# An RWKV-7 and convolution block on one core: the program writes TensorE's order itself, and a step of the recurrence takes both heads in one product

## The chip, the core and the metric

The kernel runs on one NeuronCore of a Trainium2 chip. Five engines work beside each other: TensorE (PE, matrix products; PEld is its weight load), VectorE (DVE), ScalarE (ACT), GpSimd (POOL) and SyncE (SP, which here only issues DMAs). Each runs its own instructions in the order in which they stand in the program, and waits on semaphores for the others. The metric is the device time of one execution in microseconds (us), as the median of several runs.

## The reference, cut to what matters

One block over 512 tokens and 1024 channels. Cut down, with the names of the reference:

```python
h = rms_norm(x, pre_mix_norm)
p_r, p_k, p_v, p_c, z_rwkv, z_conv = split(h @ w_in)          # 1024 x 7168
# RWKV-7: 16 heads of 64 channels; per token and head, with a state S (64 x 64):
sa = S @ a_t
S = S * w_t + outer(sa, b_t) + outer(v_t, k_t)
y = S @ r_t                                                    # a scan over 512 tokens
y_rwkv = (group_norm(y) + bonus) * g @ w_rwkv_out
# convolution: 31 taps along the tokens, one filter per channel
c = conv31(u * sigmoid(gate)); y_conv = silu(layer_norm(c)) @ w_conv_out
x = x + rms_norm((sigmoid(z_rwkv) * y_rwkv + sigmoid(z_conv) * y_conv) @ w_out)
h = rms_norm(x)
x = x + rms_norm((silu(h @ ffn_w_gate) * (h @ ffn_w_up)) @ ffn_w_down)
```

## The kernel before

Channels lie on the partitions in 8 tiles of 128 (two heads each), tokens on the free axis. A **dense product** is one 128-channel tile of an output: each operand is split into a high and a low part in fp32r, so that for each of the 8 k-tiles there are three matmuls of 128x512 (`acc3`, L179 to L181), 24 in all, into a PSUM tile `dn`. The weights come by DMA in halves (`wload`); ACT and DVE or POOL split them into `wh` and `wl`.

The scan is done in chunks of 64 tokens, for one channel tile ct (heads E and O, on partitions 0 to 63 and 64 to 127) after another. Everything of the recurrence is in plain fp32, for which one matmul in the code is two passes of TensorE; the profile counts passes. Per channel tile:

- `plan_decay`, `plan_keys`, `plan_recept`: decay, keys and receptance (`zw`, `za`, `ss`, `bck` on TensorE), then the operands `AR` and `bk`, and `bkT` by transposes (`tps`).
- `plan_inner`: 16 products `gps` give the masked matrices inside the chunks, `Mt` and `GR`.
- `plan_solve`: the inverse of I - M. DVE transposes `Mt` into `Mo` (L622), takes 31 steps of two instructions (`tt`, L634, and `Ps`, L638), and transposes back into `P` and `P32T` (L650). Small products of 32x32 (`wps`, `xps`) join the blocks; ACT writes the result into `Pbd`.
- `plan_values`: `vps`, `bps`, and the buffers `UV` and `SV`.
- `plan_chain`: the recurrence over the 8 chunks. A chunk is a row of steps in which TensorE's product goes through ACT to the next one: `zt` from `SV` and `AR`, ACT copies it to `zs` (L721), `zt` from `zs` and `Pbd`, ACT copies to `UV` (L738), `zt` from `UV` and `bkT` (and the old state through the identity), ACT scales it into the next `SV` (L751). Each product stands there twice, for E and for O, in a part of TensorE's array: `128*64` in the profile is an operand of 128 rows and 64 columns, `64*64` one of 64 and 64, `128*128` the whole array. The output `yp` of a chunk takes four more.
- `plan_finish`: group norm, bonus and gate (`ssy`, `bcy`, `gp`).

The convolution's 31 taps per channel tile are DVE instructions of 128x512 (`ca`, L844). After the scan come the gates, `w_ro`, `w_co` (operand `CH`), then the output projection (operand `MH`) and the feed-forward part (`FHH`, `FH`).

What sets the order: each piece of work is put into a list with a nominal time (`at`, with `PERIOD`, `CHT`, `CHP`, `CHS`, `SOLVE` and so on), the list is sorted, and the code is emitted in that order. Below it a scheduling layer orders the instructions of every engine once more, at build time, by its own estimate of when each is ready. Solve steps and taps are tied to each other on DVE in the order of emission.

Of the kernel before, what the change touches and what calls it, by code (L numbers as in the profile page):

```python
# [32 lines left out]
# nominal positions that order the program  # L33
PERIOD = 44.0
NCL = 3
CPERIOD = 96.0
CPERIOD2 = 20
DTZ = 0.25
CONV0 = 60
TG_ = 25  # L40
WBF = 4
T0P = 0.0
T1P = 475
TE0 = -26.0
TN0 = -10
DTC = 0.3
POST = 8
TZO = 20
LEAD = 11
DTF = 0.9  # L50
SOLVE = 25.0
CH0 = -2
CHP = 5.5
CHS = 0.9
# [44 lines left out]
def tile_hybrid_block(ctx, tc, xT, cst, prm, dwp, wl1, w2g, w_in, w_ro, w_co, w_o,  # L99
# [3 lines left out]
    PE = nc.tensor  # L103
# [96 lines left out]
    def bcast2(ps, r8, rx):  # L200
        S.activation(out=rx.rearrange("p (a v) -> p a v", v=HD),
                     in_=r8.unsqueeze(2).to_broadcast([P, 8, HD]), func=AF.Copy)
        bcast(ps, lambda b: rx[:, b * P:(b + 1) * P])

    # 1 / sqrt(v) for v > 0: a first guess from the bits, then Newton's steps
# [19 lines left out]
    def all_rstd(ps_all, eps, blocks=4):  # L225
        red = sp.tile([P, blocks], F32, tag="st", bufs=6, name="red")
        V.tensor_reduce(out=red, in_=ps_all[:, :, :, 0], axis=AX.X, op=ALU.add)
        r = rstd_from(red, eps, blocks)
# [44 lines left out]
    # mean square of x over the channels, per token  # L273
# [10 lines left out]
    # the first products take x before its norm, and the norm after them  # L284
# [26 lines left out]
    # derived parameters  # L311
# [25 lines left out]
    # low-rank inputs: (h + (h_prev - h) mu) W = h (W - mu W) + h_prev (mu W)  # L337
# [17 lines left out]
    def low_rank(g):  # L355
        t_ = low[g]
        lo_f = tmp("lo_f", "th") if g else ep_.tile([P, T], F32, name="lo_f")
        if g == 0:
            pa, pb_ = (pm.tile([P, T], F32, tag=g_, bufs=1, name="lora") for g_ in ("sb", "fi"))
            for k in range(NT):  # L360
                for q, ps in ((0, pa), (2, pb_)):
                    acc3(ps, t_[:, q, k, :], t_[:, q + 1, k, :], [k], lambda k: XH[:, k, :],
                         lambda k: XL[:, k, :], k == 0, k == NT - 1)
            sh = tmp("sh", "sq", 2)
            V.tensor_mul(lo_f, pa, bx)
            V.tensor_mul(sh, pb_, bx)
            V.tensor_add(lo_f[:, 1:T], lo_f[:, 1:T], sh[:, 0:T - 1])
            S.activation(out=lo_f[E], in_=lo_f[E], func=AF.Tanh)
            # the low parts beside the high ones, under the other half of the rows
            for X, R, Q in ((LH, E, O), (LL, O, E)):  # L370
                S.activation(out=X[R], in_=lo_f[R], func=AF.Copy)
                V.tensor_sub(X[Q], lo_f[R], f(X[R]))
        else:
            ps = pd.tile([P, T], F32, tag="dn", name="lora")
            for k in range(NT):
                for q, rh, rl in ((0, hh, hl), (2, hhs, hls)):
                    acc3(ps, t_[:, q, k, :], t_[:, q + 1, k, :], [k], rh, rl,
                         k + q == 0, k == NT - 1 and q == 2)
            S.activation(out=lo_f, in_=ps, func=AF.Tanh, scale=0.5)
            S.activation(out=lo_f, in_=lo_f, func=AF.Identity, scale=0.5, bias=0.5)  # L380
            split(lo_f, GH, GL)

    def open_loop():
# [3 lines left out]
        for j in range(2):  # L387
            t_ = kp.tile([P, NCH, L], F32, tag=f"Pbd{j}", bufs=1, name=f"Pbd{j}")
            G.memset(t_, 0.0)
            Pbd.append(t_)  # L390
# [20 lines left out]
    def low2(ps, h_, l_, R, X):  # L411
        PE.matmul(ps, lhsT=h_, rhs=X, start=True, stop=False)
        PE.matmul(ps, lhsT=l_[R], rhs=X[R], start=False, stop=True)

    st = [{} for _ in range(NT)]
    plan = []
# [7 lines left out]
    solved, tapped = [None], [None]  # L424

    halves = []

    def plan_dense(t0, dt, wap, then, rh=hh, rl=hl):
# [5 lines left out]
        def mm(k):  # L434
            if k == 0:
                d["ps"] = pd.tile([P, T], F32, tag="dn", name="dn")
            k0 = k // WK * WK
            wh, wl = d[k0]
            j = k - k0
            cols = slice(j * P, (j + 1) * P)  # L440
            acc3(d["ps"], wh[:, cols], wl[:, cols], [k], rh, rl, k == 0, k == NT - 1)

        for k0 in range(0, NT, WK):
            ts = [t0 + 3 * dt * k for k in range(k0, k0 + WK)]
            fns = [lambda k=k: mm(k) for k in range(k0, k0 + WK)]
            if k0 + WK == NT:
                ts.append(t0 + 3 * dt * NT)
                fns.append(lambda: then(d["ps"]))
            halves.append([ts, lambda eng, k0=k0: load(k0, eng), fns])

    # weights are loaded ahead of their use, as far as the buffers go
    def plan_halves():
        halves.sort(key=lambda e: e[0][0])
        for i, (ts, ld, fns) in enumerate(halves):
            t_ = ts[0] - LEAD
            if i >= WB:
                t_ = max([t_] + [e[0][WK - 1] + 0.001 for e in halves[:i - WB + 1]])
            at(0, t_)(lambda ld=ld, i=i, t_=t_: ld(G if T0P < t_ < T1P else None))
            late = max(t_ + 0.001 - ts[0], 0.0)
            ts[:] = [t + late for t in ts]  # L460
            for t, fn in zip(ts, fns):
                at(0, t)(fn)

    at(0, -36.0)(load_rest)
    at(0, -35.0)(lambda: low_weights(0))
    at(0, -30.0)(lambda: low_rank(0))
    at(0, TN0)(normed)
    at(0, 0.0)(open_loop)
    at(0, 4.0)(lambda: low_weights(1))
    at(0, TG_)(lambda: low_rank(1))  # L470

    DT = PERIOD / 72 * DTF
    DL = 24 * DT
    CHT = max(2 * DL + 14.0 + SOLVE, 3 * DL + 4.0) + CH0

# [7 lines left out]
    def plan_decay(ct):  # L483
        s_ = st[ct]

        @at(ct, 0.0)
        def _():
            w2h, w2l = low_out(ct, 0, 2 * P, "w2")
            # decay: log w = -exp(-1/2) sigmoid(z)
            zw = pm.tile([P, T], F32, tag="sm", name="zw")  # L490
            low2(zw, w2h[:, 0:P], w2l[:, 0:P], E, LH)
            cum = ktmp("cum")
            S.activation(out=cum, in_=zw, func=AF.Tanh, scale=0.5, bias=der(D_W0H, ct))
            S.activation(out=cum, in_=cum, func=AF.Identity, scale=0.5, bias=0.5)
            V.tensor_tensor_scan(out=cum, data0=reset, data1=cum, initial=0.0,
                                 op0=ALU.mult, op1=ALU.add)
# [687 lines left out]
```

## Time and profile before

| | |
|---|---|
| three runs | 1139.59, 1144.58, 1146.76 us; median 1144.58 |
| profiled execution, first to last instruction | 1165.1 us |
| busy: PE, DVE, ACT, POOL | 1138.6, 721.4, 616.5, 96.2 us |
| mean granted TensorE clock of the profiled execution | 0.950 |

The profiled execution has no time of its own outside the profiler; its span, 1165.1 us, stands 1.8% above the median of the runs without a profile. A clock of 1.00 is 2.4 GHz, 0.50 is 1.2 GHz, the two levels that are granted. Matmuls overlap in TensorE, so that the time of one more matmul is seen from the distance of two starts and not from its length.

### The profile page before, as it was taken

Reading aid. Unit: us, or ns where it says so; the run is one execution under the profiler, and the core shown is the slowest. Engines: PE = TensorE matmul, PEld = TensorE weight load, DVE = VectorE, ACT = ScalarE, POOL = GpSimd, SP = SyncE. Lnnn points to the kernel's source line nnn. Section 1 sums busy time; section 2 is a strip of 40 time slices with the busy share of each in tenths; the row PEclk is TensorE's granted clock in tenths of the full one; section 3 lists DMA queues with packets and bytes.
Section 4 is the critical chain, followed back from the end, with each engine's and each line's share of the span. In section 5 each row is a group of like instructions: output and inputs, shape, how many; then the busy total and the mean of one; then the engine's idle time right before and its main releaser. Section 6 shows DMA issues by size and latency. Waiting matters only on the chain.

```text
span 1165.1 us, 17942 instructions
## 1 busy us (share of the span) xinstructions
PE 1138.6 (98%) x6506; PEld 869.8 (75%) x6506; DVE 721.4 (62%) x1699; ACT 616.5 (53%) x1291; POOL 96.2 (8%) x140
## 2 busy tenths in 40 slices
PE   7999999999999999999999999999999999999996
PEld 5777675757676767677788788899888888888886
DVE  7968676747776748699698737546444444433324
ACT  6777776758756747564655724535333333333321
POOL 0111010101010101112222000000000000000000
PEclk9999988869988869899999999999999999999998
DMA  7145342524342423356798434500332322333322
GB/s 245 44 100 118 78 98 46 116 46 92 71 100 50 97 69 81 68 125 147 163 203 197 117 99 139 178 19 10 101 98 91 99 91 94 96 91 109 109 64 73
DMA packets 74202, 117.41 MB, mean 101 GB/s; under 512 B 15745, under 2 KB 21249, under 8 KB 74113
## 3 DMA queue, kind: packets, MB, share of 16 engines
q1 hardware_dynamic: 58848, 88.47, 25.2%
q0 software_dynamic: 15264, 27.79, 14.3%
q8 instruction: 51, 0.84, 0.3%
q14 instruction: 39, 0.31, 0.1%
HBM read 84.25 MB, written 2.10 MB: 74 GB/s over the span
## 4 chain that ended last, share of the span: by engine, by line
PE 91%; ACT 4%; DVE 3%; issue 1%; DMA 0%; SPq 0%; DVEq 0%; ACTq 0%
PE dn L179 22%; PE dn L181 22%; PE dn L180 22%; PE gps L589 3%; PE yp L759 2%; PE zt L726 2%; PE zt L718 2%; PE vps L695 1%; PE zt L744 1%; PE yp L763 1%; PE bps L704 1%; PE ss L194 1%; PE psf L180 1%; PE psf L179 1%; PE psf L181 1%
## 5 line engine op out<-in xcount | busy, mean ns | idle before, releaser
L159 ACT ACTIVATE wh<-wf 128x512 fp32r<-128x512 f32 (+1 forms) x172 | 106.6, 621 | 245.5 <-PE dn L180 237.8
L160 DVE TENSOR_TENSOR wl<-wf,wh 128x512 fp32r<-128x512 f32 (+1 forms) x172 | 116.0, 676 | 136.1 <-ACT wh L159 136.1
L179 PE MATMUL dn<-HH,wh 128*128 128x512 f32 x408 | 173.0, 426 | 0.8 <-DVE cpad L823 0.5
L844 DVE SCALAR_TENSOR_TENSOR ca<-cpad,dw,ca 128x512 f32<-128x512 f32 x240 | 171.8, 744 | 1.4
L180 PE MATMUL dn<-HL,wh 128*128 128x512 f32 x408 | 172.1, 422 | 0.0
L181 PE MATMUL dn<-HH,wl 128*128 128x512 f32 x408 | 171.1, 420 | 0.0
L170 POOL DMA_DIRECT2D wl<-wf x106 | 91.6, 870 | 505.3 <-ACT wl L169 325.6
L181 PE MATMUL dn<-FHH,wl 128*128 128x512 f32 x320 | 127.0, 397 | 0.0
L179 PE MATMUL dn<-FHH,wh 128*128 128x512 f32 x320 | 126.6, 395 | 0.0
L180 PE MATMUL dn<-FHL,wh 128*128 128x512 f32 x320 | 125.8, 393 | 0.0
L168 ACT ACTIVATE wh<-wf 128x512 fp32r<-128x512 f32 x106 | 66.3, 629 | 69.1 <-PE dn L180 68.1
L179 PEld LDWEIGHTS dn<-HH,wh 128*128 128x128 f32 x408 | 78.9, 194 | 18.9 <-issue 0.7
L181 PEld LDWEIGHTS dn<-HH,wl 128*128 128x128 f32 x408 | 78.6, 193 | 17.6 <-issue 0.5
L180 PEld LDWEIGHTS dn<-HL,wh 128*128 128x128 f32 x408 | 79.0, 194 | 16.4 <-issue 0.4
L180 PEld LDWEIGHTS dn<-FHL,wh 128*128 128x128 f32 x320 | 60.2, 188 | 15.0
L181 PEld LDWEIGHTS dn<-FHH,wl 128*128 128x128 f32 x320 | 60.1, 188 | 14.5
L179 PEld LDWEIGHTS dn<-FHH,wh 128*128 128x128 f32 x320 | 60.0, 188 | 13.8
L169 ACT ACTIVATE wl<-wh 128x512 fp32r<-128x512 f32 x106 | 66.3, 628 | 2.1 <-ACT UV L738 0.4
L179 PE MATMUL dn<-FH,wh 128*128 128x512 f32 (+1 forms) x166 | 64.3, 387 | 0.0
L181 PE MATMUL dn<-FH,wl 128*128 128x512 f32 (+1 forms) x166 | 64.1, 386 | 0.0
L180 PE MATMUL dn<-FH,wh 128*128 128x512 f32 (+1 forms) x166 | 64.1, 386 | 0.0
L638 DVE TENSOR_TENSOR Ps<-Ps,tt 128x60 f32<-128x60 f32 (+24 forms) x248 | 52.6, 212 | 3.4
(303 smaller groups left out, 2111.0 us busy)
## 6 DMA issues: line engine op xcount, KB each, us to landing
wf<-in_w_in_dram SPq DMA_DIRECT2D x112, 256.0 KB, 3.1
wl<-wf POOLq DMA_DIRECT2D x106, 256.0 KB, 3.7
wf<-in_w_gt_dram SPq DMA_DIRECT2D x44, 256.0 KB, 2.6
wf<-in_w_up_dram SPq DMA_DIRECT2D x44, 256.0 KB, 2.8
wf<-in_w_dn_dram SPq DMA_DIRECT2D x40, 256.0 KB, 2.7
wf<-in_w_ro_dram SPq DMA_DIRECT2D x16, 256.0 KB, 3.0
wf<-in_w_co_dram SPq DMA_DIRECT2D x16, 256.0 KB, 2.6
wf<-in_w_o_dram SPq DMA_DIRECT2D x16, 256.0 KB, 2.9
```

What stands on the lines that cost most here:

```text
L159: S.activation(out=hi, in_=src, func=AF.Copy)
L160: V.tensor_sub(lo, src, f(hi))
L168: S.activation(out=wh, in_=wf, func=AF.Copy)
L169: S.activation(out=wl, in_=f(wh), func=AF.Copy, scale=-1.0)
L170: G.dma_start(out=wl, in_=wf, accum_op=ALU.add)
L179: PE.matmul(ps, lhsT=a, rhs=rh(k), start=first and j == 0, stop=False)
L180: PE.matmul(ps, lhsT=a, rhs=rl(k), start=False, stop=False)
L181: PE.matmul(ps, lhsT=b, rhs=rh(k), start=False, stop=last and j == n - 1)
L589: PE.matmul(ps[:, c, :], lhsT=bk[R, hc * 4 + c, :], rhs=AR[R, hc * 4 + c, par:par + 2, :], start=True, stop=True)
L638: solved[0] = V.tensor_add(Ps[:, 0:j, q0:8], Ps[:, 0:j, q0:8], tt)
L718: PE.matmul(zt[R, 0, :], lhsT=AR[:, c, 2 * par, :], rhs=SV[:, c, par, :], start=True, stop=True)
L844: a_ = V.scalar_tensor_tensor(out=o_, in0=cb[:, j:j + T], scalar=tap(j), in1=o_, op0=ALU.mult, op1=ALU.add)
```

## The change

1. All matmuls from the start of the recurrence to the merge get a dependency on the one before them (class `Pinned`), so that TensorE's order is the order in which the code emits them and nothing moves it. `Pinned` also adds up a nominal TensorE clock `PE.t`.
2. The list of nominal times is gone. Each channel tile has generators (`prep`, `values`, `chain`, `taps`, `finish`), which yield a delay or an event to wait for; `Weave` resumes whichever is due at `PE.t`, and otherwise emits the three matmuls of one k-tile of a dense product whose weights are taken to be loaded.
3. A chain step takes both heads in one product of the whole array: `AR` holds both heads' operands next to each other, `Pbd` is block-diagonal with 128 columns, and the state comes out as two 64-column halves, of which ACT takes the diagonal blocks. ACT copies `zs` in two instructions where it was one.
4. The outputs `yp` are taken after chunk 4 and after chunk 8 instead of in each chunk.
5. `zw` and `za` use full-height low parts, padded with zeros. The 32 `gps` passes of a tile come after the solve of the tile before it, where they could begin earlier. `low_rank` of the gate stands ahead of the first keys.

```diff
+    class Pinned:
+        on, last, t, mode = False, None, 0.0, None
+        def _pin(self, i, lhsT, rhs, tr=False):
+            if self.on and self.last is not None:
+                order(i, self.last)
+            self.last = i
...
+            if self.mode not in (None, mode):
+                self.t += 0.12
...
-    def at(ct, t):
-        def add(fn):
-            plan.append((ct * PERIOD + t, len(plan), fn))
-            return fn
-        return add
+    class Weave:
...
+        def run(self):
+            while True:
+                if self.heap and self.heap[0][0] <= PE.t:
+                    self.step(heapq.heappop(self.heap)[2])
+                    continue
+                self.feed()
+                if self.loaded and self.loaded[0][0] <= PE.t:
+                    units = self.loaded[0][1]
+                    units.pop(0)()
...
-            zt = pc.tile([P, 3, L], F32, tag="ch", name="zt")
-            for par, R in ((0, E), (1, O)):
-                PE.matmul(zt[R, 0, :], lhsT=AR[:, c, 2 * par, :], rhs=SV[:, c, par, :],
-                          start=True, stop=True)
-            zs = sp.tile([P, L], F32, tag="zs", name="zs")
-            S.activation(out=zs, in_=zt[:, 0, :], func=AF.Copy)
...
+            zt = pc.tile([P, 5, L], F32, tag="ch", name="zt")
+            PE.matmul(zt[:, 0:2, :], lhsT=AR[:, c, 0:2, :], rhs=SV[:, c, :, :],
+                      start=True, stop=True)
+            zs = sp.tile([P, L], F32, tag="zs", name="zs")
+            for par, R in ((0, E), (1, O)):
+                S.activation(out=zs[R], in_=zt[R, par, :], func=AF.Copy)
+            yield HOP
+            PE.matmul(zt[:, 2, :], lhsT=pb[:, c, :], rhs=zs, start=True, stop=True)
...
+                if c > 0:
+                    PE.matmul(zt[:, 3:5, :], lhsT=ident, rhs=SV[:, c, :, :],
+                              start=True, stop=False)
+                PE.matmul(zt[:, 3:5, :], lhsT=bkT[:, c, :], rhs=UV[:, c, :, :],
+                          start=c == 0, stop=True)
...
+            if c == NCH // 2 - 1:
+                yp = s_["yp"] = py.tile([P, NCH, L], F32, tag="y", name="yp")
+                outputs(range(0, NCH // 2))
+            if c < NCH - 1:
+                yield HOP
+        outputs(range(NCH // 2, NCH))
...
+        if ct:
+            yield ("solve", ct - 1), 0.0
+        Mt = kp.tile([P, NCH, L], F32, tag="Mt", bufs=BUFS[4], name="Mt")
```

On TensorE, in the chain of a channel tile, before. `zt` are the products of the steps, `dn` the dense ones, `x2` is one for each head:

```order
L726 MATMUL zt<-zs,Pbd_486 64x64 x2
L730 MATMUL zt<-SV,cs 64x64 x2
L180 MATMUL dn<-HL,wh 128x512
L181 MATMUL dn<-HH,wl 128x512
L744 MATMUL zt<-UV,bkT 64x64 x2
L763 MATMUL yp<-GR,UV 64x64 x2
L179 MATMUL dn<-HH,wh 128x512
L180 MATMUL dn<-HL,wh 128x512
L759 MATMUL yp<-AR,SV 64x64
L718 MATMUL zt<-SV,AR 64x64 x2
L759 MATMUL yp<-AR,SV 64x64
L181 MATMUL dn<-HH,wl 128x512
```

The same place after the change (all matmuls have the line of `Pinned.matmul`, transposes that of `Pinned.transpose`):

```order
L115 MATMUL zt<-SV,cs 128x128
L115 MATMUL zt<-UV,bkT 128x128
L115 MATMUL dn<-HH,wh 128x512
L115 MATMUL dn<-HL,wh 128x512
L115 MATMUL dn<-HH,wl 128x512
L115 MATMUL dn<-HH,wh 128x512
L115 MATMUL dn<-HL,wh 128x512
L115 MATMUL dn<-HH,wl 128x512
L115 MATMUL zt<-SV,AR 128x128
```

Six dense matmuls now stand between two steps where one to three stood, one product where there were two, and the outputs are gone from between them.

On TensorE, from the end of a solve on, before (`wps` is the first product that needs the solve, `gps` the one that the next solve needs):

```order
L659 MATMUL wps<-P32T,Mt 32x32 x16
L180 MATMUL dn<-HL,wh 128x512
L181 MATMUL dn<-HH,wl 128x512
L179 MATMUL dn<-HH,wh 128x512
L180 MATMUL dn<-HL,wh 128x512
L670 MATMUL xps<-P_2202,Wt 32x32 x16
```

After the change, behind the solve of the fifth channel tile:

```order
L115 MATMUL wps<-P32T,Mt 32x32 x16
L115 MATMUL yp<-AR,SV 64x64 x8
L115 MATMUL yp<-GR,UV 64x64 x8
L115 MATMUL vps<-cs,mu_v 128x128 x4
L115 MATMUL xps<-P_3700,Wt 32x32 x16
L115 MATMUL ssy<-cs,sqy 128x16 x4
L118 MATMUL tps<-cs,bk 128x128 x4
L115 MATMUL zt<-SV,AR 128x128
L118 MATMUL tps<-cs,bk 128x128 x4
L115 MATMUL zt<-zs,Pbd_505 128x64
L115 MATMUL gps<-AR,bk 128x128 x8
```

Here dense matmuls are gone from between `wps` and `xps`, and other small products stand in their place; `xps` can't be passed by anything any more.

On DVE, in a solve after the change (`ca` is a tap):

```order
L673 TENSOR_TENSOR tt<-Mo,Ps 128x54
L677 TENSOR_TENSOR Ps<-Ps,tt 128x27x2
L673 TENSOR_TENSOR tt<-Mo,Ps 128x52
L677 TENSOR_TENSOR Ps<-Ps,tt 128x26x2
L857 SCALAR_TENSOR_TENSOR ca<-cpad_96,dw,ca 128x512
```

Two solve steps and a tap alternate through nearly the whole solve, where before a solve had 9 taps and more of the other work.

## Rows read from the trace of the kernel before

**Rows 1.** First page: span, and the busy times.

```profile
span 1165.1 us, 17942 instructions
PE 1138.6 (98%) x6506; PEld 869.8 (75%) x6506; DVE 721.4 (62%) x1699; ACT 616.5 (53%) x1291; POOL 96.2 (8%) x140
```

**Rows 2.** Windows: stretch, length, busy time (instructions) by engine, clock, DMA.

```profile
40.00:110.00 70.00, 66.90 (x380) 51.04 (x380) 55.95 (x154) 53.34 (x101) 11.35 (x19) 1.00 0.42 92
110.00:500.00 390.00, 385.39 (x2748) 261.44 (x2748) 261.58 (x855) 261.33 (x654) 47.23 (x69) 0.86 0.36 78
574.40:731.20 156.80, 156.00 (x694) 126.53 (x691) 113.29 (x187) 83.65 (x140) 19.83 (x23) 1.00 0.61 153
731.20:1165.10 433.90, 423.98 (x2080) 352.67 (x2078) 196.26 (x346) 151.41 (x261) 0.00 (x0) 0.99 0.29 88
```

**Rows 3.** Windows around the longest stretch at the low clock, TensorE alone.

```profile
222.00:225.60 3.60, 3.59 (x32) 1.00 0.29 77
225.70:233.00 7.30, 7.30 (x42) 0.50 0.44 90
233.00:253.00 20.00, 20.00 (x95) 0.50 0.13 24
253.00:263.00 10.00, 10.00 (x80) 1.00 0.37 86
```

**Rows 4.** Windows: a stretch of the feed-forward part, dense products alone.

```profile
873.90:903.00 29.10, 29.10 (x127) 23.45 (x126) 14.40 (x22) 9.99 (x16) 0.00 (x0) 1.00 0.28 91
```

**Rows 5.** Timeline of TensorE in a chain, full clock: start, length, instruction.

```profile
184.18 0.39 PE L181 MATMUL dn<-HH,wl 128*128 128x512 f32 x1
184.50 0.33 PE L726 MATMUL zt<-zs,Pbd 64*64 64x64 f32 x4
184.66 0.28 PE L730 MATMUL zt<-SV,cs 64*64 64x64 f32 x4
184.87 0.50 PE L179 MATMUL dn<-HH,wh 128*128 128x512 f32 x1
185.21 0.39 PE L180 MATMUL dn<-HL,wh 128*128 128x512 f32 x1
```

**Rows 6.** Timeline of TensorE, small products in the whole array, full clock.

```profile
66.88 1.05 PE L695 MATMUL vps<-cs,mu_v 128*128 128x128 f32 x8
67.69 0.48 PE L179 MATMUL dn<-HH,wh 128*128 128x512 f32 x1
```

**Rows 7.** Timeline of TensorE, small products at the low clock.

```profile
228.02 1.22 PE L695 MATMUL vps<-cs,mu_v 128*128 128x128 f32 x4
228.90 0.77 PE L412 MATMUL zw<-LH,w2h 128*128 128x512 f32 x1
```

**Rows 8.** Windows of three solves, Mo's end to P32T's, and sum of all seven.

```profile
229.40:280.40 51.00, 51.00 (x287) 32.76 (x286) 30.21 (x114) 30.99 (x74) 5.59 (x9) 0.77 0.31 67
293.10:331.40 38.30, 38.30 (x267) 26.47 (x265) 30.08 (x114) 27.44 (x65) 4.88 (x9) 1.00 0.38 83
467.20:509.70 42.50, 42.50 (x259) 28.24 (x260) 29.99 (x103) 21.50 (x55) 6.06 (x7) 0.91 0.42 87
sum 310.50, PE 309.68 PEld 206.28 DVE 211.52 ACT 196.65 POOL 37.68; mean PE 44.24 PEld 29.47 DVE 30.22 ACT 28.09 POOL 5.38
```

**Rows 9.** Lines L622 (Mo) and L650 (P32T): ns, first to last start.

```profile
L622 DVE STREAM_TRANSPOSE Mo<-Mt x8: 1908/1927/1965, 78.5 to 465.3; 128x1024 f32<-128x1024 f32 x8
...
L650 DVE STREAM_TRANSPOSE P32T<-P x8: 434/440/464, 105.8 to 509.3; 128x256 f32<-128x256 f32 x8
```

**Rows 10.** Groups on ACT, 60 to 620 us: busy, mean ns, idle before.

```profile
L666 ACT ACTIVATE Pbd<-P 32x256 f32<-32x256 f32 x32 | 13.2, 414 | 3.5 <-DVE P L647 3.1
L699 ACT ACTIVATE UV<-vps 64x256 f32<-64x256 f32 x32 | 12.0, 376 | 2.4 <-PE vps L695 2.0
L662 ACT ACTIVATE Wt<-wps 32x256 f32<-32x256 f32 x16 | 6.0, 377 | 0.5
```

**Rows 11.** Group on DVE: the taps of the convolution, first page.

```profile
L844 DVE SCALAR_TENSOR_TENSOR ca<-cpad,dw,ca 128x512 f32<-128x512 f32 x240 | 171.8, 744 | 1.4
```

More of the change, by code (lines that the diff above doesn't have):

```diff
@@ L1 @@
+import heapq
 import math
@@ L356, in low_rank @@
         t_ = low[g]
[L357 to L381, printed above, removed]
@@ L429, in plan_dense, with dense_tile @@
+    wv = Weave()
+    def dense_tile(wap, then, rh=hh, rl=hl, need=(), ev=None):
         d = {}
@@ L436, in mm, with halves @@
                 d["ps"] = pd.tile([P, T], F32, tag="dn", name="dn")
[L437 to L440, printed above, removed]
+            wh, wl = d[k // WK * WK]
+            cols = slice(k % WK * P, (k % WK + 1) * P)
             acc3(d["ps"], wh[:, cols], wl[:, cols], [k], rh, rl, k == 0, k == NT - 1)
[L443 to L474, printed above, removed]
+            if k == NT - 1:
+                then(d["ps"])
+                if ev:
+                    wv.post(ev)
+        def halves():
+            return [(lambda eng, k0=k0: load(k0, eng),
+                     [lambda k=k: mm(k) for k in range(k0, k0 + WK)]) for k0 in range(0, NT, WK)]
+        wv.items.append((need, halves))
     def low_out(ct, c0, n, nm):
@@ new lines, in prep @@
+        wv.post(("keys", ct))
+        yield 3.0
+        bkT = kp.tile([P, NCH, P], F32, tag="bkT", bufs=BUFS[2], name="bkT")
+        for hc in range(2):
+            ps = pm.tile([P, 4, P], F32, tag="sm", name="tps")
+            for c in range(4):
+                PE.transpose(ps[:, c, :], bk[:, hc * 4 + c, :], ident)
+            S.activation(out=bkT[:, hc * 4:hc * 4 + 4, :], in_=ps, func=AF.Copy)
+            yield 0.7
+        yield ("r", ct), 1.6
+        tr = s_["tr"]
+        V.tensor_mul(AR[:, :, 2, :], ch3(tr), ep[:, :, 1:L + 1])
@@ L631, in step @@
+        yield 1.5
+        for j in range(B32 - 1, 0, -1):
             q0 = j // 4
@@ new lines, in prep @@
+        R1 = [slice(h * 64, h * 64 + 32) for h in range(2)]
+        R2 = [slice(h * 64 + 32, h * 64 + 64) for h in range(2)]
+        ps = pm.tile([P, NCH, B32], F32, tag="sb", bufs=1, name="wps")
+        for c in range(NCH):
+            for h in range(2):
+                PE.matmul(ps[R2[h], c, :], lhsT=Mt[R1[h], c, B32:L], rhs=P32T[R1[h], c, :],
+                          start=True, stop=True)
+        for h in range(2):
+            S.activation(out=Wt[R2[h]], in_=ps[R2[h]], func=AF.Copy)
@@ new lines, in prep @@
+        pb = Pbd[ct % 2]
+        for h in range(2):
+            for j, R in enumerate((R1[h], R2[h])):
+                S.activation(out=pb[R, :, h * L + j * B32:h * L + (j + 1) * B32], in_=P32[R],
+                             func=AF.Copy)
+        yield 1.4
+        ps = pm.tile([P, NCH, B32], F32, tag="sb", bufs=1, name="xps")
+        for c in range(NCH):
+            for h in range(2):
+                PE.matmul(ps[R1[h], c, :], lhsT=Wt[R2[h], c, :], rhs=P32[R2[h], c, :],
+                          start=True, stop=True)
@@ L875, in tile_hybrid_block, with middle @@
     mid = {}
-    @at(0, TM)
-    def _():
+    def middle():
+        yield ("chain", NT - 1), 0.0
         ctx_w.close()
```

715 lines of the change are left out of this document (380 added, 335 removed).

## Prediction, as it stood before the run

> **What bounds the kernel now.** I read the first page, then windows by stage, then the timeline of TensorE. TensorE is busy for 1138.6 of 1165.1 us, and no other engine for more than 62% [rows 1]; in the stretch that holds nearly the whole recurrence it is idle for under 5 of 390 us [rows 2]. So the kernel is bound by TensorE, and the question is what its busy time is made of. Three things in it are not dense products at full rate.
>
> First, the clock. From 110 to 500 us the mean granted clock is 0.86 [rows 2]; with the two levels of 1.00 and 0.50 that is 0.28 of 390 us, or 109 us, at 1.2 GHz, in six stretches. The longest is typical: for 3.6 us ahead of it TensorE ran only small products, in tiles of the array, one after another; it fell at 225.7 us and rose again only at 253 us, when dense and small products had alternated for a while [rows 3]. If everything in those 109 us were bound by columns, 54 us could be won at most.
>
> Second, changes of the array's shape. A dense matmul follows the one before it after 29.1 us / 127 = 0.229 us [rows 4]. Where the next product is one in tiles, the distance is 184.50 - 184.18 = 0.32 us, so 0.09 us for the change; from tiles back to the whole array it is 184.87 - 184.66 = 0.21 against 0.16 between two kinds of the same shape, about as much (both intervals hold four passes); the first dense product afterwards takes 0.34 instead of 0.23 [rows 5]. The program has 583 such changes before.
>
> Third, the small products themselves. Two heads' products in tiles, four passes, take 184.66 - 184.50 = 0.16 us [rows 5].
>
> After 731 us comes work that the change leaves alone, 433.9 us [rows 2]; it takes no part in the sum.
>
> **The change, part by part.** *Shapes.* In the changed order TensorE's shape changes 108 times, 475 fewer: 475 x 0.09 = 43 us at full clock. Returns from small to dense products fall from 236 to 200 only, so the 0.1 us behind them gives 4 us more.
>
> *One product for two heads.* 464 products of `zt` in tiles, 232 pairs at 0.16 = 37 us, become 232 of the whole array, two passes each. The nearest rows for a whole-array pass of 128 columns are the `vps`, (67.69 - 66.88) / 8 = 0.10 us [rows 6]: 232 x 0.20 = 47 us, 10 us more. The range is small: 0.16 for a product (nothing lost) to 0.25 (20 us lost).
>
> The row shows 0.16 us for two heads in tiles and 0.20 us for both in the whole array [rows 5, 6]. The Trainium skill, TensorEngine Tiling (Array Packing), section Theoretical Speedup, gives tiles up to a factor of 2 where one dimension is 64; by that the 37 us would become 74 instead of 47, and the result 27 us later. The rows speak against it.
>
> So TensorE's own work gets about 37 us shorter at full clock. That would be the answer if its order stayed as full as it is. It doesn't: the rest of the sum is about waits.
>
> *The pinned order.* Before, whatever is late is passed by dense products. Now a late small product holds everything behind it. In the middle of a chain this is covered: six dense matmuls, 6 x 0.229 = 1.4 us, stand between two steps, against ACT's copy and one operation in front of it. It is not covered between two solves. I cut the recurrence into solves (from the end of `Mo` to the end of `P32T`, on DVE) and stretches between them, in which TensorE must do the small products from `wps` to the last `gps`.
>
> Before, the first `Mo` ends at 80.4 and the last `P32T` at 509.7 us. The second to the eighth solve take 310.5 us, 44.4 each; the first takes 25.8 [rows 8, 9]. For the seven stretches between 429.3 - 336.3 = 93 us are left, 13.3 each. The solves are longer the lower the clock: 38.3 us at 1.00, 51.0 at 0.77, with the same 30 us of DVE work [rows 8].
>
> After, by the order:
>
> - Start. The same until 40 us; then 156 dense products and small ones worth some 10 us stand ahead of the last `gps` of the first tile, against less work before, since `low_rank` now comes first: 40 + 36 + 10 + 4 of idle and copies = 90, and the first `Mo` ends at 92 instead of 80.4 us (3.1 us of idle in 70 are from [rows 2]).
> - Solves. DVE has the same 62 solve instructions, 17 taps instead of 9, six fewer other operations of 128x512 and ten fewer tiny ones. A tap takes 0.744 us, and the others are of the same size [rows 11]; that cancels to within 2 us, so DVE's 30 us stay [rows 8]. TensorE has 81 to 111 dense matmuls and 8 to 10 us of small ones in a solve, 29 to 34 us, and 2 us of returns. Both are below the 38.3 us that the best solve took. I take 35.5 for each of the six in the middle, 34 for the first, 28 for the last with its 75 dense matmuls. The floor is DVE's 30, the other end is 40, near the mean of before.
> - Between the solves. TensorE has 9, 0, 15, 9, 0, 15 and 0 dense matmuls there, and of small ones, behind the fifth solve for example, 60 passes of `vps`, `ssy`, `tps`, `bcy`, `gps` and 10 of `zt` at 0.10 us, six of 512 columns at four times that, and about 3 us of tiles: 12 to 13 us at full clock. On top come waits that were filled before: `xps` waits for `Wt`, and ACT has four `UV`, four `Pbd` and two `Wt` to do, 4 x 0.376 + 4 x 0.414 + 2 x 0.377 = 3.9 us [rows 10]; the last `gps` wait for their buffers, and `Mo` itself takes 1.9 [rows 9]. That makes 18 at full clock. At the low clock the same small products take twice as long: four passes of `vps` 228.90 - 228.02 = 0.88 us, 0.22 each [rows 7], so up to 28. These stretches are what the clock fell in before [rows 3], and I expect it to fall again shortly after each `wps`. I take 24.
> - End. From the last `wps` to the merge TensorE has 741 dense matmuls, 170 us, some 12 us of small ones and 8 us of waits: 190, where it took 731.2 - 509.7 = 221.5 [rows 2, 8]. This is the gain that is safe: the longer stretches before it have taken in more dense work.
>
> Sum: 92 + 34 + 7 x 24 + 6 x 35.5 + 28 + 190 = 725 us against 731.2. So 6 us less in the profiled execution, which would make 1159; by the 1.8% between it and the runs [rows 1], **1138 us**, 0.6% under the median. The 37 us of saved TensorE work and the part of the 54 us of clock that comes back inside the chains are spent on waits between the solves.
>
> *The rest.* ACT's 64 extra copies of `zs` hide under the six dense matmuls of a step; without that cover they'd be under 64 x 0.376 = 24 us, by ACT's larger copies [rows 10]. Outputs in two batches stand outside the steps and cost the same passes. 56 taps are left after the last solve instead of 133, 37 us of DVE beside 50 us of chain: no wait at the layer norm.
>
> **The rivals.** *The order holds, and the clock stays up* (for it: at 1.00 a solve took 38.3 us even with fewer dense products between the steps; against it: four of seven stretches between solves have at most nine dense matmuls, three none). Then the stretches between take 18, the solves 35, the end 188: 92 + 34 + 126 + 210 + 29 + 188 = 679, 52 us less, **1092 us** by the same ratio.
>
> *TensorE is held at `wps` by the solve on DVE* (slower). TensorE is through its 29 to 34 us before DVE is through with the taps and the steps; it then stands still at `wps`, with nothing to pass it, the clock falls before the stretch begins instead of in it, and all of the small products run at 1.2 GHz. For it: DVE's 30 us of work took 38 us at best [rows 8]; against it: DVE's waits for TensorE, of which those 8 us were made, get shorter too. Price: 26 between, 39 for a solve, 31 for the last, 38 for the first, 193 at the end: 92 + 38 + 182 + 234 + 31 + 193 = 770, 39 us more, **1183 us**. It decides from about 61 us for a solve and a stretch together; I have 59.5, before it was 57.7.
>
> *A whole-array product costs as much as the page's factor of 2 says*: 27 us on top, **1165 us**; the `vps` row leaves it little room.
>
> *The change doesn't do what it says.* The order shows the shapes, the products and the dense matmuls where the description has them; what could differ is only the time.
>
> **How the numbers follow.** The forecast, a band of 1118 to 1157 us around 1138, has 0.46, the first rival 0.26 (1075 to 1118), the second 0.24 (1157 to 1205), the third 0.04. A measurement of this kernel can tell about 1% from no change, 11.4 us: below 1133 is faster, above 1156 slower. Two fifths of the forecast's band lie below 1133, a twentieth above. So faster 0.26 + 0.18 = 0.44, slower 0.24 + 0.04 + 0.02 = 0.30, the same 0.26. To leave out a tenth at either end the range goes from 1088, near the first rival's middle, to 1184, the second's.
>
> **What would show it.** Right: shape changes gone and TensorE's matmuls between 110 and 500 us fewer, yet idle time of TensorE there no longer under 5 us but 40 or more, ended by ACT (`Wt`, `Pbd`, `zs`) and DVE (`P32T`, `bcy`'s inputs); low clock in every stretch from `wps` to the last `gps` and not inside the chains; the first `Mo` near 90, the merge's end near 725. If the low stretches are gone, the first rival holds; if the longest idle of TensorE ends at `wps` by `P32T`, the second. I would be wrong altogether if steps inside the chains waited too, because ACT has loads in front of a copy: 192 steps at 0.2 us would be 38 us more.

## The result, and the profile after

The changed kernel takes 1190.1 us (median of 4 runs, 1185.6 to 1193.4) against 1144.6 us: a ratio of 1.038, 95% interval 1.033 to 1.043. Forecast were 1138 us, at most 1184.

The first page after, answering to [rows 1]:

```profile
span 1187.8 us, 17114 instructions
PE 1087.9 (92%) x6042; PEld 886.7 (75%) x6042; DVE 735.2 (62%) x1708; ACT 636.6 (54%) x1354; POOL 96.2 (8%) x140
```

TensorE is busy for 51 us less than before and idle for 99.9 us instead of 26.5. The windows of the same kernel, from the first `Mo` to the last `P32T`, to the last `yp`, to the merge's end, and the rest (stretch, length, busy time by engine, clock, DMA):

```profile
90.60:532.80 442.20, 381.84 (x2565) 306.73 (x2564) 350.43 (x1040) 306.10 (x756) 58.17 (x83) 0.87 0.39 85
532.80:594.40 61.60, 57.12 (x413) 46.59 (x411) 45.28 (x73) 40.66 (x104) 12.30 (x15) 0.97 0.59 129
594.40:754.00 159.60, 146.85 (x631) 118.44 (x630) 74.92 (x130) 77.31 (x128) 16.34 (x19) 0.95 0.52 133
754.00:1187.80 433.80, 423.49 (x2078) 352.26 (x2076) 195.82 (x346) 151.11 (x261) 0.00 (x0) 0.99 0.29 87
```

In the first, 60 of 442 us are idle, where [rows 2] show 5 of 390; the last is as long as before. The instructions that mark the stretches (duration least/median/most, first to last start), beside [rows 9]:

```profile
L663 DVE STREAM_TRANSPOSE Mo<-Mt x8: 1891/2008/2027, 88.6 to 505.4; 128x1024 f32<-128x1024 f32 x8
...
L683 DVE STREAM_TRANSPOSE P32T<-P x8: 428/439/450, 123.5 to 532.4; 128x256 f32<-128x256 f32 x8
...
L115 PE MATMUL dn<-CH,wl x64: 392/393/398, 709.5 to 753.4; 128*128 128x512 f32 x64
```

From one `Mo` to the next it takes (505.4 - 88.6) / 7 = 59.5 us; before it was 55.3. What TensorE waits for (total, times, longest):

```profile
PE wps L115 <- DVE P32T L683: 14.1, 4, 5.9
PE bcy L118 <- ACT rxy L218: 13.5, 3, 7.0
PE xps L115 <- ACT UV L728: 10.4, 3, 4.4
PE zt L115 <- ACT SV L781: 7.5, 9, 2.1
PE zt L115 <- ACT zs L767: 7.2, 8, 1.6
PE zt L115 <- ACT UV L771: 7.2, 7, 1.9
...
PE dn L115 <- ACT T L946: 5.7, 2, 5.1
```

TensorE's timeline between two solves shows one of them, at `xps`:

```profile
357.56 0.69 PE L115 MATMUL wps<-P32T,Mt 32*32 32x32 f32 x32
358.18 0.68 PE L115 MATMUL yp<-AR,SV 64*64 64x64 f32 x16
358.79 0.80 PE L115 MATMUL yp<-GR,UV 128*64 128x64 f32 x16
360.48 1.16 PE L115 MATMUL vps<-cs,mu_v 128*128 128x128 f32 x8 [0.89 <-ACT Wt L696]
366.02 1.06 PE L115 MATMUL xps<-P,Wt 32*32 32x32 f32 x32 [4.38 <-ACT UV L728]
```

`vps` and `xps` share one buffer (tag `sb`, one of it), so `xps` waits until ACT has copied `vps` out. ACT's timeline says what stands ahead of that:

```profile
361.30 1.27 ACT L613 ACTIVATE AR<-kkn 64x512 f32<-64x512 f32 x2
362.48 0.61 ACT L615 ACTIVATE bk<-cum 64x512 f32<-64x512 f32 x1
363.10 0.60 ACT L797 ACTIVATE sqy<-yp 128x512 f32<-128x512 f32 x1
363.71 0.69 ACT L799 ACTIVATE ys<-yp,pr 128x512 f32<-128x512 f32 x1
364.41 1.56 ACT L728 ACTIVATE UV<-vps 64x256 f32<-64x256 f32 x4
```

From 358.2 to 367 TensorE has no dense product. The chain step, where dense products do stand, at full clock:

```profile
346.74 0.39 PE L115 MATMUL dn<-HH,wl 128*128 128x512 f32 x1
346.96 0.38 PE L115 MATMUL zt<-SV,cs 128*128 128x128 f32 x2
347.18 0.39 PE L115 MATMUL zt<-UV,bkT 128*128 128x128 f32 x2
347.32 0.48 PE L115 MATMUL dn<-HH,wh 128*128 128x512 f32 x1
347.64 0.40 PE L115 MATMUL dn<-HL,wh 128*128 128x512 f32 x1
```

A wide product takes 0.14 to 0.22 us, without a shape change ahead of it (0.22 from the dense one); the first dense one behind it 0.32.

### The profile page after: what moved, and what is told of

Its sections match the earlier page's. It is cut to its first block, busy times and chain, and to the rows that moved or that the text cites. A ratio compares the mean times of both kernels' runs of the same rounds, so it can differ in the third digit from the quotient of the medians.

```text
span 1187.8 us, 17114 instructions
## 1 busy us (share of the span) xinstructions
PE 1087.9 (92%) x6042; PEld 886.7 (75%) x6042; DVE 735.2 (62%) x1708; ACT 636.6 (54%) x1354; POOL 96.2 (8%) x140
## 4 chain that ended last, share of the span: by engine, by line
PE 79%; ACT 10%; DVE 8%; issue 2%; DMA 1%; SPq 0%; DVEq 0%; ACTq 0%
PE dn L115 60%; PE zt L115 4%; PE gps L115 2%; PE psf L115 2%; DVE ca L857 2%; PE wo L115 1%; PE lora L115 1%; PE yp L115 1%; PE tps L118 1%; PE bps L115 1%; PE ssy L115 1%; ACT SV L781 1%; ACT wh L185 1%; ACT wl L186 1%; PE xps L115 1%
## 5 line engine op out<-in xcount | busy, mean ns | idle before, releaser
L176 ACT ACTIVATE wh<-wf 128x512 fp32r<-128x512 f32 x173 | 107.0, 621 | 242.9 <-PE dn L115 238.5
L177 DVE TENSOR_TENSOR wl<-wf,wh 128x512 fp32r<-128x512 f32 x173 | 116.3, 676 | 135.7 <-ACT wh L176 135.6
L115 PE MATMUL dn<-HH,wh 128*128 128x512 f32 x408 | 182.4, 447 | 5.1 <-ACT T L946 5.1
L857 DVE SCALAR_TENSOR_TENSOR ca<-cpad,dw,ca 128x512 f32<-128x512 f32 x240 | 178.8, 745 | 2.3
L115 PE MATMUL dn<-HL,wh 128*128 128x512 f32 x408 | 166.5, 408 | 0.0
L115 PE MATMUL dn<-HH,wl 128*128 128x512 f32 x408 | 165.5, 406 | 0.0
L115 PE MATMUL dn<-FH,wh 128*128 128x512 f32 (+1 forms) x332 | 101.0, 387 | 0.0
L185 ACT ACTIVATE wh<-wf 128x512 fp32r<-128x512 f32 x105 | 66.1, 630 | 60.3 <-PE dn L115 59.2
L115 PEld LDWEIGHTS dn<-FH,wh 128*128 128x128 f32 x332 | 61.5, 188 | 13.7
```

The lines of the kernel that those rows point to most:

```text
L115: return self._pin(nc.tensor.matmul(out, lhsT=lhsT, rhs=rhs, **k), lhsT, rhs)
L176: S.activation(out=hi, in_=src, func=AF.Copy)
L177: V.tensor_sub(lo, src, f(hi))
L185: S.activation(out=wh, in_=wf, func=AF.Copy)
L857: a_ = V.scalar_tensor_tensor(out=o_, in0=cb[:, j:j + T], scalar=tap(j), in1=o_, op0=ALU.mult, op1=ALU.add)
```

## The experiments

The theory (1): the loss is in waits that the pinned order doesn't fill, since its nominal times are shorter than the answers of ACT and DVE, and in the low clock that goes with them. Rivals: the wide products and the outputs cost more (2); the new order of the program costs, pinned or not (3); a wait taken out comes back at the next product, since a recurrence sets the pace (4); the loss is behind the last solve (5); it is in the chain steps (6).

The median is of the device times; the ratio is to the kernel before, run beside it. Period: first to last start of `Mo`, over 7. Idle: span less TensorE's busy time on the first page. Clock: mean granted clock of the profiled span. The runs of the kernel before have medians from 1143.0 to 1154.5 us beside the different experiments, so differences under 1% between two rows are not clear of noise.

| kernel | us | ratio (95%) | period | idle | clock |
|---|---|---|---|---|---|
| before, as profiled | 1144.6 | 1 | 55.3 | 26.5 | 0.950 |
| after | 1190.1 | 1.038 (1.033 to 1.043) | 59.5 | 99.9 | 0.941 |
| b_wide | 1146.1 | 1.002 (0.999 to 1.005) | 53.2 | 28.4 | 0.987 |
| b_both | 1129.0 | 0.987 (0.981 to 0.994) | 51.2 | 32.6 | 0.987 |
| a_free | 1127.9 | 0.989 (0.982 to 0.996) | 56.1 | 38.5 | 0.982 |
| a_tiles | 1205.4 | 1.056 (1.050 to 1.062) | 60.7 | 96.1 | 0.951 |
| a_sb | 1186.9 | 1.030 (1.021 to 1.040) | 59.6 | 102.0 | 0.950 |
| a_newton | 1192.3 | 1.035 (1.028 to 1.042) | 60.4 | 100.1 | 0.940 |
| a_mend | 1208.4 | 1.051 (1.043 to 1.059) | 62.8 | 118.4 | 0.936 |
| a_hop | 1197.7 | 1.046 (1.038 to 1.054) | 60.9 | 106.5 | 0.942 |
| f_newton | 1129.8 | 0.981 (0.974 to 0.988) | 55.2 | 40.7 | 0.991 |
| pin_tail | 1150.1 | 1.005 (1.001 to 1.009) | 54.3 | 59.6 | 0.976 |
| pin_head | 1175.0 | 1.027 (1.018 to 1.037) | 59.1 | 87.8 | 0.947 |
| pin_chain | 1142.3 | 0.997 (0.995 to 0.999) | 54.8 | 61.0 | 0.960 |
| pin_stretch | 1178.7 | 1.029 (1.023 to 1.035) | 57.8 | 93.8 | 0.955 |
| f_norm | 1120.6 | 0.979 (0.974 to 0.983) | 54.5 | 35.1 | 0.993 |

**The products and the outputs without the pin.** `b_wide` puts the wide chain products into the kernel before, `b_both` the two batches of outputs too.

```diff
-                PE.matmul(zt[R, 0, :], lhsT=AR[:, c, 2 * par, :], rhs=SV[:, c, par, :],
+            PE.matmul(zt[:, 0:2, :], lhsT=AR[:, c, 0:2, :], rhs=SV[:, c, :, :],
...
+            if c == NCH // 2 - 1:
+                outputs(range(0, NCH // 2))
```

> The kernel before with one part of the change alone: a chain step takes both heads in one 128x128 product; the order stays the old one, with each output product in its own chunk. Theory 1 (the loss is in waits: in the pinned order nothing can pass a late small product, so TensorE idles and its clock falls; the wide products are cheap): 133 shape changes fewer at 0.09 us are 12 us, the wide products cost up to 10 us more, so 1125 to 1145 us, and idle of TensorE between 110 and 731 us stays under 12 us. Rival 2 (the wide product itself, with its two copies of zs, is what costs): over 1155 us, by longer chains.

> The kernel before with two parts of the change, wide chain products and outputs in two batches, and the old order: 301 shape changes instead of 583. Theory 1: 282 x 0.09 = 25 us less for shapes, up to 10 us more for wide products: 1118 to 1138 us, TensorE's idle still under 15 us. Rival 2 (wide products and batches cost): over 1155 us.

`b_wide` is level with before, 1 us above Theory 1's range; `b_both` is 1.3% faster, inside it. Rival 2 falls: the products don't cost 45 us.

But `b_wide` is level for another reason than the theory gives. An estimate of TensorE's work at full clock is the span times its mean clock (a low stretch counts half), less the idle time: 1165.1 x 0.950 - 26.5 = 1080 us before, 1144.4 x 0.987 - 28.4 = 1101 us in `b_wide`. That is 21 us more where the theory has 2 less, and a higher clock hides it. In `b_both` it is 1128.2 x 0.987 - 32.6 = 1081 us, as before, where the theory has 15 less. So in the old order the wide products cost more than the 10 us that the theory allows, or a shape change gives back less than 0.09 us; no run here tells which.

**The pin alone.** `a_free` is the changed kernel with its order left to the scheduler.

```diff
-    PE.on = True
```

What the pin had kept in order by itself is tied in this kernel, and in the others below that are wholly or partly without a pin: the outputs of a tile to each other, and the product of the old state between the two beside it.

> The changed kernel with its pin taken away: the program is written in the same order, but only accumulations are tied, and the scheduler sets TensorE's order (272 shape changes instead of 108). Theory 1: idle of TensorE between 110 us and the merge falls from 77 to under 20 us, the time to 1115 to 1145 us. Rival 3 (the new order of the program, with its loads and lags, is what costs, pinned or not): it stays over 1170 us. Rival 2 (wide products): over 1170 us too, but with little idle time.

62 us come back, as Theory 1 said; rivals 2 and 3 fall. The profiled execution was the slowest of its four (1136.9 us at a clock of 0.982; the others 1124.2 to 1128.8 us at 0.988 to 0.994). Its first page and its windows from the first `Mo` to the last `P32T`, to the last `yp`, to the merge's end:

```profile
span 1135.1 us, 17072 instructions
PE 1096.6 (97%) x6042; PEld 866.8 (76%) x6042; DVE 717.0 (63%) x1708; ACT 635.5 (56%) x1354; POOL 96.4 (8%) x140
```

```profile
89.60:514.80 425.20, 413.95 (x2701) 309.01 (x2700) 337.61 (x1048) 320.82 (x791) 64.52 (x90) 0.96 0.45 97
514.80:551.30 36.50, 35.91 (x273) 25.90 (x271) 29.41 (x49) 25.29 (x71) 6.03 (x7) 1.00 0.50 111
551.30:701.20 149.90, 144.15 (x631) 116.50 (x632) 85.86 (x147) 77.15 (x128) 16.37 (x19) 0.99 0.56 144
```

The same stretch behind `wps` in its timeline has dense products in each gap:

```profile
347.99 0.69 PE L115 MATMUL wps<-P32T,Mt 32*32 32x32 f32 x32
348.61 0.50 PE L115 MATMUL dn<-HH,wh 128*128 128x512 f32 x1
...
350.13 1.16 PE L115 MATMUL vps<-cs,mu_v 128*128 128x128 f32 x8
351.05 0.48 PE L115 MATMUL dn<-HH,wl 128*128 128x512 f32 x1
...
353.74 0.69 PE L115 MATMUL xps<-P,Wt 32*32 32x32 f32 x32 [0.82 <-ACT UV L728]
```

From `wps` to `xps` 5.8 us pass, against 8.5 in the pinned order, and ahead of `xps` TensorE idles for 0.8 us instead of 4.4.

**Tiles in the pinned order.** `a_tiles` keeps the pin and takes each chain product per head.

```diff
-            PE.matmul(zt[:, 0:2, :], lhsT=AR[:, c, 0:2, :], rhs=SV[:, c, :, :],
+            for par, R in ((0, E), (1, O)):
+                PE.matmul(zt[R, par, :], lhsT=AR[:, c, par, :], rhs=SV[:, c, par, :],
```

> The changed kernel, still pinned, but a chain step takes the two heads' products in tiles again, as before: 470 shape changes instead of 108. Theory 1: TensorE's work grows by 362 x 0.09 = 33 us less up to 10 us, of which a part goes into waits: 1200 to 1220 us. Rival 2 (wide products cost more than tiles): faster than the changed kernel, under 1180 us.

15 us slower than the changed kernel, with 362 more shape changes: in this order the wide products are a gain.

**Single waits ahead of the last solve.** `a_sb` puts `vps` behind `xps`; `a_newton` holds a root's tiny operations together on DVE; `a_hop` lengthens the nominal hop of a chain; `a_mend` joins the first two with a longer nominal solve.

In `a_sb` and `a_mend`, ahead of `vps`:

```diff
         yield ("v", ct), 1.6
+        if ct:
+            yield ("solve", ct - 1), 0.0
```

In `a_newton` and `a_mend` at each tap, and likewise at each split and at the sums ahead of the layer norm:

```diff
-            if solved[0] is not None:
-                order(a_, solved[0])
+            for b_ in (solved[0], newton[0]):
+                if b_ is not None:
+                    order(a_, b_)
```

In `a_hop`, and in `a_mend`:

```diff
-HOP = 1.35
+HOP = 1.75
...
-SOLVE = 22.0
+SOLVE = 26.0
```

> The changed kernel, pinned, with one wait taken out: the vps of the next tile come behind xps in the program, so that xps no longer waits until four UV copies have emptied the buffer it shares with vps. Theory 1 (waits in the pinned order are the loss): the three waits of 10.4 us at xps for UV are gone, and with them a part of the low clock that follows: 1170 to 1184 us. Rival 4 (a wait taken out in a pinned order comes back at the next product, because the values are later): within 5 us of the changed kernel's 1190.

> The changed kernel, pinned, with another wait shortened: on DVE the taps and splits written behind the ten tiny operations of a root stay behind them, where they now stand between them at 0.7 us each. Theory 1: the waits at bcy and bck for their rows (16 us in the trace) fall under 5 us, and the low clock behind the longest goes too: 1166 to 1182 us. Rival 4: the time comes back at later taps, solve steps or hops: within 5 us of 1190.

> The changed kernel, pinned, with the nominal time between two products of a chain set to 1.75 instead of 1.35: nine dense matmuls stand there instead of six. Theory 1 (each wait costs what it shows): the 22 us of waits of zt products for ACT go, 1165 to 1182 us. Rival 4 (the length of the recurrence per channel tile is what counts in a pinned order, and what is added to a chain makes it longer): 24 steps x 3 x 0.23 us = 17 us per tile are more than the 3 us of waits there, and 1195 us or more.

> The changed kernel, pinned, with both waits taken out and the nominal time of a solve set to 26 instead of 22, so that more dense products stand ahead of wps. Theory 1: idle of TensorE between 110 us and the merge falls from 77 to 40 us or less, and the time to 1135 to 1165 us. Rival 4: above 1175 us.

All four times go with rival 4, but only `a_sb` is a test of it. There the three waits at `xps` for `UV` are gone, and the last `P32T` ends at 533.5 us all the same, where it ended at 532.8: TensorE idles for 66 us from the first `Mo` to there instead of 60. Other waits have grown:

```profile
PE zt L115 <- ACT SV L783: 12.3, 13, 2.1
...
PE vps L115 <- ACT Pbd L709: 7.1, 5, 2.8
PE ssy L115 <- ACT sqy L799: 4.9, 3, 2.8
```

By the time it gained 3 us; by the ratios, 1.030 against 1.038, it would be 9, and their intervals overlap, so a small gain is not excluded.

`a_newton` does on DVE what it says. DVE's timeline of the changed kernel had a tap of 0.75 us between any two of the tiny operations, from 547.2 to 555.2 us, 8 us for eleven:

```profile
547.23 0.17 DVE L804 TENSOR_SCALAR n<-ssy 128x8 f32<-128x8 f32 x1 [5.09 <-PE ssy L115]
...
554.27 0.16 DVE L228 SCALAR_TENSOR_TENSOR rw<-rt,ry 128x8 f32<-128x8 f32 x1
554.39 0.75 DVE L857 SCALAR_TENSOR_TENSOR ca<-cpad,dw,ca 128x512 f32<-128x512 f32 x1
555.06 0.16 DVE L229 SCALAR_TENSOR_TENSOR ry<-rw,ry 128x8 f32<-128x8 f32 x1
```

In `a_newton` the root of the same tile takes 2.2 us:

```profile
554.17 0.17 DVE L809 TENSOR_SCALAR n<-ssy 128x8 f32<-128x8 f32 x1 [11.68 <-PE ssy L115]
...
556.18 0.17 DVE L233 SCALAR_TENSOR_TENSOR ry<-rw,ry 128x8 f32<-128x8 f32 x1
```

And its waits:

```profile
PE wps L115 <- DVE P32T L688: 23.6, 7, 5.7
...
PE bcy L118 <- ACT rxy L222: 4.1, 1, 4.1
```

The wait at `bcy` fell from 13.5 to 4.1 us, the one at `wps` rose from 14.1 to 23.6, and TensorE's idle is unchanged at 100. But these are not the same microseconds moved on. Of the 13.5 us in the changed kernel 11.5 lay behind the last solve, at 555.9 and 605.3 us:

```profile
605.31 1.11 PE L118 MATMUL bcy<-cs,rxy 128*128 128x128 f32 x4 [7.00 <-ACT rxy L218]
```

Every wait at `wps` lies ahead of it. In `a_newton` the last `P32T` ends at 540.3 us, 7.5 later, and from there to the merge's end 215.3 us pass instead of 221.0, 5.7 less: the end gains and the solves lose.

In `a_hop` the waits at `zt` grew, from 22 to 35 us, so it takes no wait out and says nothing on what becomes of one; its period grew by 1.4 us, not by the 17 of its row. In `a_mend` the longer nominal solve put 17 to 21 taps beside the first seven solves instead of 15 to 18, which are tied to its steps; from the end of `Mo` to that of `P32T` they took 41 us on average, in the changed kernel 34.0. Two or three taps are about 2 us of that; the rest is not traced, and the waits at `zt` are 36 us there. That kernel shows that a nominal time is no lever by itself, not what a well-chosen one would do.

**Where in the program the pin costs.** `pin_tail` pins only behind the last solve's `xps`; `pin_head` has `True` and `False` the other way round and pins only up to it.

```diff
-    PE.on = True
...
         s_["pb"] = pb
+        if ct == NT - 1:
+            PE.on = True
```

> The changed kernel with the pin only behind the xps of the last solve; ahead of it only accumulations are tied. Theory 1a (the pin costs in the seven periods of solves and stretches, and the end is longer only by the waits that its own rows show): the last P32T ends near 515 as without a pin (1128 us), and the end keeps its two waits at bcy and the one at dn, 17 us of idle and some low clock: 1140 to 1155 us. Rival 5 (the end is where the pin costs most): over 1165 us.

> The changed kernel with the pin only up to the xps of the last solve. Behind it TensorE's order differs from the changed kernel's by little more than that the two bcy with their gp stand behind more dense products. Theory 1a: the two waits of 11.5 us at bcy behind the last solve go, and 5 us of low clock: 1172 to 1180 us. Rival 5: under 1160 us. Rival 4 (a wait taken out comes back elsewhere): 1186 us or more.

Both times are as Theory 1a said; rival 5 falls. In `pin_tail` that is in part luck: its last `P32T` ended at 496 us instead of 515, and its end, from there to the merge's end, took 218 us where that of `a_free` takes 186, which is more than the 17 us of idle and some low clock. In `pin_head` the two waits at `bcy` (4.5 and 7.0 us) are gone with the low clock behind them. The window from its last `P32T` to the merge's end:

```profile
530.90:737.00 206.10, 200.22 (x1036) 162.01 (x1035) 119.72 (x201) 117.38 (x232) 28.60 (x34) 0.98 0.59 141
```

With the same 758 dense matmuls that is 15 us less than in the changed kernel, 11 of them idle time, and the time falls by 15 us, run against run: behind the last solve a wait is worth what it shows, and the low clock behind it comes on top. The larger part, 47 us from `a_free` to `pin_head`, lies ahead of it.

**Where in a period.** `pin_chain` pins from the last `gps` to the next `wps`; `pin_stretch`, with `True` and `False` the other way round, from `wps` to the last `gps`. No `gps` follows the last `wps`, so `pin_stretch` stays pinned from there to the merge: against its expectation, it is not free behind the last solve.

```diff
+        PE.on, PE.last = False, None
         Wt = kp.tile([P, NCH, B32], F32, tag="Ps", bufs=1, name="Wt")
...
+        PE.on, PE.last = True, None
         wv.post(("inner", ct))
```

> The changed kernel with the pin only from a tile's last gps to the next wps, that is in the solves with their chain steps and six dense matmuls between two; from wps to the last gps, and behind the last solve, only accumulations are tied (143 shape changes; dense products now stand between wps and xps and between the gps). Theory 1b (the pin costs in the stretches between solves, where small products stand one behind another with nothing between them): the stretches fall from 25 to about 14 us each, idle between 110 us and the merge to under 30 us, low clock to under 50 us, and the time to 1100 to 1135 us. Rival 6 (it costs in the chains, by the waits of their steps for ACT): 1155 us or more.

> The opposite: pinned only from wps to the last gps of each tile, free in the solves and behind the last (150 shape changes). Theory 1b: most of the loss in the seven periods stays, 1150 to 1175 us. Rival 6: 1135 us or less.

The direction is Theory 1b's: pinning the chains alone costs 14 us over `a_free`, pinning the stretches and the end 51. That the end of `pin_stretch` is pinned its waits show, with the changed kernel's two at `bcy` behind the last solve:

```profile
PE bcy L118 <- ACT rxy L218: 11.5, 2, 7.0
```

The stretches without the end come out of `pin_chain` and `pin_head`, whose ends are both free: 1175.0 - 1142.3 = 33 us. So the 62 us of the pin, taken in this order, are 14 for the chains, 33 for the stretches and 15 for the end.

Both missed their numbers, `pin_chain` by 7 us and `pin_stretch` by 4; the latter is less than its pinned end costs. `pin_chain` also missed the rest of its row: between 110 us and the merge it has 38 us of idle for under 30 and 82 us of low clock for under 50. From the seven ends of `P32T` to the next `Mo`'s, stretches take 25.5 us in the changed kernel, 23.5 in `pin_stretch`, 19.9 in `pin_chain` and 15.7 in `a_free`; the first seven solves 34.0, 34.4, 34.9 and 40.4. So with a pin in either place a solve is 5 to 6 us shorter, and the stretches get longer by 4 us with the chains pinned and by 8 with the stretches pinned; the pinned chain still has 18 us of waits at its `zt` and a clock of 0.96. In `pin_stretch` TensorE runs through the dense products of the solve too early and then stands at `wps`:

```profile
PE wps L115 <- DVE P32T L684: 33.6, 6, 8.1
```

**A better kernel.** `f_newton` is `a_free` with the root held together; `f_norm` is `a_free` with the layer norm's last tiles in four portions.

```diff
             split(ca[:, k, :], CH[:, k, :], CL[:, k, :])
+            if k % 2:
+                yield 6.0
```

> The changed kernel without its pin (1128 us), and with the tiny operations of a root held together on DVE. Theory 1: without the pin other products stand ahead of bcy, so the wait is covered already and the time stays within 1% of 1128. Rival 4 (DVE's order sets the length of a chain whatever TensorE's order): 1112 us or less.

> The changed kernel without its pin (1128 us), and with the layer norm's last eight tiles written in four portions, so that the sigmoid of a gate isn't queued behind all of them on ACT: in the trace without the pin one dense product waits 5.1 us for it. Theory 1c (behind the recurrence, where nothing recurs, a wait is worth what it shows): the wait goes and the time falls by 3 to 6 us, to 1120 to 1126 us. Rival 4 (it comes back elsewhere; ACT loads its tables more often): 1128 us or more.

`f_newton` stays where it was: without the pin other products cover the root. `f_norm` is the fastest, 2.1% below before. The wait of 5.1 us at the sigmoid `T` is 0.7 in it:

```profile
PE dn L115 <- ACT T L954: 0.7, 1, 0.7
```

Its time lies in the range, at the lower edge, and its gain, 7.3 us, is above the 3 to 6 that were forecast. A part of it is clock: `a_free`'s fastest run, at 0.994, took 1124.2 us, and `f_norm` at 0.993 takes 1121.5, 2.7 less.

## Why the prediction was wrong

**TensorE's own work: right in the pinned order.** It was to shrink by 37 us at full clock; busy time shrank by 51, at a lower clock. Counted from start to start without the idle time, and low stretches at half, the work is 1034 us instead of 1084, 50 less. The wide product, put at 0.20 us, took 0.14 to 0.22. By the Trainium skill, TensorEngine Tiling (Array Packing), section Theoretical Speedup, whose factor of up to 2 for tiles was the third rival, `a_tiles` could have been faster than the changed kernel. It is 15 us slower, though with 362 more shape changes, so that no run here shows the factor by itself. The two terms one by one are not borne out elsewhere: in the old order, `b_wide` and `b_both`, the work grew by 21 us and by 1 where they have 2 and 15 us less.

**Up to the last solve: right in its length, in part by luck.** First `Mo` 92 us forecast, 90.6 measured; a solve and the stretch behind it 59.5, measured 59.5 (the stretches 25.5 for 24, the six middle solves 34.1 for 35.5); last `P32T` at 535, measured 532.8. That the saved work would be spent on waits is what `a_free` shows, and that the pin costs most in the stretches, `pin_chain` and `pin_head`. As forecast, the clock is low in each of the seven stretches, 84 of 113 us. But of the 60 us of idle only 26 lie in the stretches, where the prediction put the waits; 35 lie in the solves, 14 of them at `wps` for `P32T` and 15 in the steps of the chains. I had called the steps covered, and had said that I would be wrong altogether if they waited; they waited 22 us, of the 38 that I had named. The middle solves came out near 35.5 us because two misses cancel: TensorE's work in them is 30 us at full clock instead of 31 to 36, and 4 us are idle where I had none.

**The end: wrong by 31 us.** "This is the gain that is safe", 190 us; it took 754 - 532.8 = 221. The 758 dense matmuls, 741 forecast, took 180 us at full clock instead of 170, at 0.237 us each instead of 0.229; small products 17 instead of 12; idle was 17 us instead of 8, in the two waits at `bcy` and the one at `dn` for `T`; and the low clock, which I didn't have there (20 us of it, at a mean of 0.97 and 0.95), makes up the remaining 7. I had looked at the length of the chain of ACT and DVE in each stretch between solves, but not in the end, where a root on DVE (8 us beside taps) and a sigmoid behind sixteen operations on ACT stand ahead of a pinned product. `pin_head`, whose end isn't pinned, gains 15 of the 31 us; `f_norm`, which takes the wait at the sigmoid out, gains up to 7 over `a_free`.

**The step from the trace to the runs: wrong by 21 us.** I took the 1.8% between the profiled execution and the median [rows 1] for the price of profiling, and made 1138 of 1159. But the profiled runs of the other kernels lie among their own runs, each with a time 1.7 to 2.3 us above its span. What set that one execution of before apart was its clock: 0.950 over 1165.1 us. In 62 runs of before beside the experiments the span goes from 1133.1 us at 0.981 to 1171.0 at 0.942, with a median of 1145.1; only 11 are over 1155 us. So much of the 109 us of low clock that I read was its own, and the changed kernel had to be set against 1144.6 - 1.8 - 433.9 = 709, not 731 us, up to the merge.

**The rivals.** The second gave 1183 us, but by another road: TensorE does wait at `wps`, 14.1 us in four places, the largest sum of its waits (the longest single one, 7.0 us, is at `bcy`), but solves took 34, not 39, and its period of 65 us did not come. The first, a clock that stays up, is what the unpinned kernels do.

**Where the gain without the pin comes from.** At (1 - 0.968) / 0.5 x 1148 = 73 us, the run of before with the median time beside `f_norm` was at 1.2 GHz, and `f_norm` for 16 at 0.993. Half of the difference is 29 us; 27 were gained. So the clock can account for all of it. Span times clock says the same: 1103 to 1114 us in the 62 runs of before, 1119.8 x 0.993 = 1112 in `f_norm`, 1135.1 x 0.982 = 1115 in `a_free`. The fewer shape changes there, 272 for 583, are not seen in the time. Why the clock stays up in these orders is open: no run here holds the clock apart from the order.

## What to carry to other kernels

An order that a program writes from nominal times is as good as the longest late answer in it. Look for the stretches in which small products wait for one another through other engines, and keep dense products there; a chain whose steps are already apart needs them less. In a recurrence that sets the pace, a wait that is taken out can come back at the next products, as in `a_sb`, so sum the loop, not the waits; behind it a wait counted for itself. Before a kernel's gain is put down to its work, and before a profile's time is scaled to a median, hold the clock of that execution against the clocks of the runs.

## What the runs showed of the hardware

The same program's granted clock varies between executions: before, from 0.942 to 0.981 in 62 runs beside the experiments, with spans of 1171.0 and 1133.1 us, and 0.950 in the profiled one. In the changed kernel low stretches go with idle TensorE. The first, of 20.5 us:

```profile
116.40:136.90 20.50, 13.92 (x100) 9.58 (x99) 13.36 (x31) 9.09 (x22) 0.86 (x1) 0.50 0.15 39
```

Ahead of it and in its beginning, from 112.2 to 124.0 us, TensorE did only `tps` and two `bps` between waits of 3.2 and 5.9 us. If the waits brought the clock down, a wait is paid again in the products behind it. They are not needed for it: before, the clock fell behind 3.6 us of small products between which TensorE didn't idle [rows 3]. Which of the two did it here, no run tells apart.
